# Ten small DRAM transfers per layer move from SyncE's queue to ScalarE's, and the planner's rules for them change

## The chip, the cores and the metric

The kernel runs on one core of a Trainium2 chip. The metric is the device time of one execution in microseconds. An execution uses five engines: TensorE (PE, matrix products; its weight loads are shown apart as PEld), VectorE (DVE), ScalarE (ACT), GpSimd (POOL) and SyncE (SP). SP does no arithmetic here: its instructions issue DMA transfers. A DMA can be issued from ACT's instruction stream as well.

## The reference, cut to what matters

The program is two layers of two blocks each over 256 tokens of 1024 features. Block 1 has differential attention, a gated delta rule in both directions and an MLP, all behind an adaLN vector; block 2 has windowed attention and experts. The change sits in the gated delta rule, which needs the inverse T of a unit lower triangular matrix of 64 by 64 for every head, chunk and direction:

```python
decay = jnp.where(incl, jnp.exp(jnp.where(incl, gdiff, 0.0)), 0.0)
kb = k * beta[..., None]
L = jnp.where(strict, jnp.einsum('bhncd,bhnmd->bhncm', kb, k) * decay, 0.0)
T = lax.linalg.triangular_solve(eye + L, jnp.broadcast_to(eye, L.shape), left_side=True,
                                lower=True, unit_diagonal=True)
u = jnp.einsum('bhncm,bhnme->bhnce', T, v * beta[..., None])
w = jnp.einsum('bhncm,bhnmd->bhncd', T, kb * jnp.exp(g)[..., None])
...
(then a scan over the chunks with u, w and a state)
```

## The kernel before, in words

All products with weights run in two fp32r halves. Weights come in units of 1 MB by `SY.dma_start`; ACT rounds a half of a unit (128x1024) to its high part, DVE subtracts it to get the low part, and PE takes both in products written `ps<-quarter,block` in the profile. A unit thus needs two ACT and two DVE operations before PE can use all of it. These operations are called hi splits and lo splits below.

The inverse is computed in `deltanet` in these steps, once per layer:

- C^T, the strict triangle, comes from two DVE products (one per direction, `quarter<-quarter,quarter`). Four DMAs write it to a DRAM tensor `lb`, one for each direction and half of the partitions.
- One DMA reads the 16x16 blocks on the diagonal back, one per partition (`w<-lb`; the tile is `lt` in the code). DVE copies them (`COPY w<-w 64x256`), and 30 small DVE products and subtractions invert them. The result and its transpose are called X; the last step is a DVE copy (`COPY quarter<-quarter 128x256`).
- One DMA writes X to a DRAM tensor `xd`, and four read it back in block diagonal form (`w<-xd`). Four DVE products make the first T of them, and PE goes from 16x16 to 64x64 blocks with products of 64 rows.

So there are ten small DMAs in a layer, twenty in all. In the kernel before they are written as `SY.dma_start`, and SP issues them in one row with the weight loads.

The order on every engine comes from a planner (`Plan`). Operations are recorded in program order; `keys` gives each its distance to the end by a schedule that runs backwards, and `schedule` then lets each engine take the ready operation with the longest way to go. Other work of the layer that does not need the inverse (gate, attention, adaLN products) is woven into the same block of operations, so a change of one key can move operations on all engines. In the kernel before, all DMAs go through one line in the planner: a DMA starts after the DMA before it is done (`dma = max(t + DMA_START, dma) + o.dma`, line 557). Block 1 of both layers is planned in this way. The order in which operations are issued is then fixed in the program; each engine runs its own row in that order and waits on semaphores.

Of the kernel before, what the change touches and what calls it, by code (L numbers as in the profile page):

```python
# [20 lines left out]
NEG = -1e30  # L21
# [11 lines left out]
# ---------------------------------------------------------------- host layout  # L33
def _units(w, n=2):
    """[K, N] -> [N/(128 n), 128 (k in chunk), n, K/128, 128]: lhsT units of n column chunks."""
    k, c = w.shape
    a = w.reshape(k // 128, 128, c // (128 * n), n, 128).transpose(2, 1, 3, 0, 4)
    return np.ascontiguousarray(a).reshape(c // (128 * n), 128, -1)


def _rows(w, kc):
    """[K, N] -> [K/(128 kc), 128, kc, N]: rhs units of kc row chunks."""
    k, c = w.shape
    a = w.reshape(k // (128 * kc), kc, 128, c).transpose(0, 2, 1, 3)
    return np.ascontiguousarray(a).reshape(k // (128 * kc), 128, -1)


def _cols(v):
    """[n*128] -> [128, n]"""
# [14 lines left out]
def _shape_consts():  # L64
    """constants of the program, packed by the time that they are needed: c0 always, c1 and c2 per block"""
# [71 lines left out]
def _bias(rpb):  # L137
    """[4, 15, 31] -> [4, 128 (q in tile), 2 * 256]: bias of q over k, NEG outside q's window"""
# [92 lines left out]
def _rows_n(w, n):  # L231
    """[1024, N] -> [N/n, 128, 8, n]"""
# [5 lines left out]
# ---------------------------------------------------------------- order of issue  # L238


class Ref:
    """an access pattern of a tile that gets its place when its operations are issued"""
# [28 lines left out]

class Tile:
# [7 lines left out]
class Plan:  # L280
    """Operations are recorded in program order and issued in the order of a list schedule: each engine takes,
    among the operations whose operands are there, the one with the longest way to the end. Costs and latencies
    are the guide's, in ns; they depend on shapes alone. A tile's slot is given out ahead of program order only if
    program order could still go on from there. Products that fill half of the array or less are not issued in long
    rows while others are ready: the array's clock falls when it is used little."""
# [17 lines left out]
    # -------------------------------------------------------- recording  # L303
    def engine(self, key, eng):
        plan = self

        class Proxy:
            def __getattr__(self, name):
                return lambda *a, **k: plan.add(key if name != "dma_start" else "S", name, getattr(eng, name), a, k)
# [16 lines left out]
    def box(r):  # L326
        """(what, partitions from, to, columns from, to)"""
# [37 lines left out]
    def add(self, eng, name, fn, args, kw):  # L365
# [4 lines left out]
        if eng == "P" and self.cols(ins[0]) < 128 and name == "matmul":  # L370
            p = self.ops[-1]
            rng = outs[0].ap.ap[0][1], outs[0].ap.offset // outs[0].ap.ap[0][0]
            if p.group and p.outs[0].t is outs[0].t and rng not in p.group:
                p.group.append(rng)
                self.access(p, n - 1, ins, outs)
                p.calls.append((fn, args, kw))
# [10 lines left out]
        o.eng, o.calls, o.dma, o.deps, o.succ, o.start, o.tiles = eng, [(fn, args, kw)], None, set(), [], None, []  # L387
        if eng == "S":
            b = self.cols(outs[0] if isinstance(outs[0], Ref) else ins[0])
            o.dma, o.dur = max(50.0, 1.4224 * b), 450.0  # L390
            if not isinstance(ins[0], Ref) and ins[0].tensor.name in self.W:
                o.dma = 3.5 * b
        else:
# [32 lines left out]
    # -------------------------------------------------------- scheduling  # L426
# [3 lines left out]
    def keys(self, n0):  # L430
        """time to the end by a list schedule that runs backwards, in which every engine is single"""
# [9 lines left out]
        for _ in range(n0, n):  # L441
# [10 lines left out]
            if o.dma:  # L452
# [12 lines left out]
    def schedule(self, slots):  # L465
        """slots: per kind of tile, the time at which each slot gets free"""
# [24 lines left out]
        def fit(e, t, dur):  # L491
            """the first time from t on at which engine e is idle for dur"""
# [8 lines left out]
        def can(i, t):  # L501
            """the earliest time from t on at which operation i's tiles have slots"""
# [16 lines left out]
        while len(order) < n - n0:  # L519
# [36 lines left out]
            if o.dma:  # L556
# [15 lines left out]
        for e, q in self.busy.items():  # L572
            q += [(ops[i].start, ops[i].end) for i in order if ops[i].eng == e]
# [5 lines left out]
    def flush(self, place, slots, issue):  # L579
        """schedules what has been recorded, into what waits and has gaps; place(kind, slot): the slot's memory"""  # L580
# [8 lines left out]
        for i, place in self.waiting:  # L589
# [5 lines left out]
            for fn, args, kw in o.calls:  # L595
# [1546 lines left out]
```

## Time and profile before

| | us |
|---|---|
| three runs | 2407.43, 2407.26, 2403.64 |
| median | 2407.26 |
| span of the profiled execution | 2408.3 |
| PE busy in it | 1984.8 (82%) |
| DVE busy | 1159.4 (48%) |
| ACT busy | 786.9 (33%) |
| POOL busy | 465.6 (19%) |

The profiled execution is known by its span alone; the span is 1.0 us above the median of the three runs. Layer 0's delta rule lies at about 140 to 340 us of the span, layer 1's at about 740 to 960 us. Block 2 starts behind the two blocks 1, at about 1330 us. All instructions of the program but the last branch stand on line 596 in this profile, because one helper issues them; so operations are told apart by engine, name and shape. The profile gives names of buffers, not those of the code: tiles of 512 columns are `quarter`, small ones `w`, weight units `block`.

### The profile page before, as it was taken

To read this page: it belongs to the slowest core of one execution; us is meant where nothing else is said; L and a number is where in the kernel's file an instruction comes from. 1 tells how busy PE (TensorE), PEld (TensorE's weight loads), DVE (VectorE), ACT (ScalarE), POOL (GpSimd) and SP (SyncE) were. 2 spreads that over 40 slices of the span, in tenths; PEclk is the share of its full clock that TensorE was granted. 3 is DMA by queue.
4 is the path that set the end of the run, shared out by engine and by line. 5 is a ranking of instruction groups with operands and counts; after the bars stand their busy time and mean duration, and the time that the engine had idled before them with its cause. 6 is when DMAs were issued, how large, how long until landed. Compare 5 with 4: busy or idle time off the path is not lost. (4 is left out here: it accounts for less than half of the span.)

```text
span 2408.3 us, 38449 instructions
## 1 busy us (share of the span) xinstructions
PE 1984.8 (82%) x16200; PEld 1437.7 (60%) x16200; DVE 1159.4 (48%) x1908; ACT 786.9 (33%) x1508; POOL 465.6 (19%) x278
## 2 busy tenths in 40 slices
PE   8688987778989999999999887666769988666665
PEld 5677777777987777999986542222237644222222
DVE  5998478999789623775557410000006731000001
ACT  4363343433457323654456210000015521000001
POOL 1555354455133312000020210000002111000000
PEclk7897898788999768999999888887779988877777
DMA  8354224566633310645544699999995579999997
GB/s 315 124 188 128 105 106 158 210 229 254 237 121 132 116 36 18 247 158 178 203 153 167 274 420 420 421 421 420 421 420 212 209 281 420 420 421 420 420 421 313
DMA packets 108253, 622.36 MB, mean 258 GB/s; under 512 B 27184, under 2 KB 28464, under 8 KB 34992
## 3 DMA queue, kind: packets, MB, share of 16 engines
q1 hardware_dynamic: 108080, 619.90, 65.4%
q8 instruction: 127, 2.08, 0.3%
q14 instruction: 46, 0.38, 0.0%
HBM read 617.24 MB, written 2.62 MB: 257 GB/s over the span
## 5 line engine op out<-in xcount | busy, mean ns | idle before, releaser
L596 PE MATMUL ps<-quarter,block 128*128 128x256 f32 (+1 forms) x5760 | 868.4, 304 | 72.5 <-DVE quarter L596 23.6
L596 PEld LDWEIGHTS ps<-quarter,block 128*128 128x128 f32 x5760 | 786.2, 205 | 114.9 <-issue 28.2
L596 PE MATMUL ps<-block,block 128*32 128x256 f32 (+4 forms) x5204 | 546.5, 431 | 137.9 <-DMA block<-in_w_up_dram 95.1
L596 PEld LDWEIGHTS ps<-block,block 128*32 128x32 f32 (+2 forms) x5204 | 274.4, 136 | 354.7 <-DMA block<-in_w_up_dram 159.3
L596 DVE TENSOR_TENSOR block<-block,block 128x1024 fp32r<-128x1024 f32 (+2 forms) x262 | 364.7, 1398 | 130.6 <-PE ps L596 73.1
L596 ACT ACTIVATE block<-block 128x1024 fp32r<-128x1024 f32 (+2 forms) x312 | 319.1, 1028 | 321.9 <-PE ps L596 292.8
L596 ACT ACTIVATE w<-ps 128x256 f32<-128x256 f32 (+1 forms) x138 | 52.3, 382 | 819.0 <-PE ps L596 818.9
L596 DVE TENSOR_TENSOR w<-w,ps 128x256 f32<-128x256 f32 x64 | 26.9, 421 | 544.3 <-ACT w L596 537.8
L596 POOL TENSOR_TENSOR block<-block,block 128x1024 fp32r<-128x1024 f32 x46 | 117.0, 2551 | 794.3 <-ACT block L596 387.8
L596 PE MATMUL ps<-block,w 128*32 128x256 f32 x2048 | 176.0, 500 | 25.8 <-ACT w L596 13.3
L596 PE MATMUL ps<-quarter,quarter 64*64 64x64 f32 (+6 forms) x1312 | 166.8, 304 | 6.9 <-DVE quarter L596 6.9
L596 PEld LDWEIGHTS ps<-block,w 128*32 128x32 f32 x2048 | 76.9, 142 | 116.2 <-issue 49.8
L596 PEld LDWEIGHTS ps<-quarter,quarter 64*64 64x64 f32 (+3 forms) x1312 | 113.2, 177 | 53.2 <-issue 20.0
L596 ACT ACTIVATE quarter<-quarter 128x512 f32<-128x512 f32 (+2 forms) x188 | 116.2, 628 | 85.0 <-DVE quarter L596 82.5
L596 ACT ACTIVATE quarter<-ps 128x512 f32<-128x512 f32 (+1 forms) x136 | 79.5, 592 | 151.2 <-PE ps L596 133.8
L596 DVE SCALAR_TENSOR_TENSOR w<-block,cT,w 128x256 f32<-128x256 f32 x140 | 126.5, 903 | 2.2
L596 DVE TENSOR_SCALAR w<-c,slot 128x256 f32<-128x256 f32 x32 | 12.5, 411 | 234.9 <-PE ps L596 234.8
L596 PE MATMUL ps<-w,w 32*128 32x256 f32 x512 | 106.7, 418 | 15.4 <-ACT w L596 15.1
L596 POOL TENSOR_TENSOR block<-block,cT 128x2048 f32<-128x2048 f32 x20 | 76.5, 3825 | 136.8 <-DVE w L596 41.0
L596 PEld LDWEIGHTS ps<-w,w 32*128 32x128 f32 x512 | 55.5, 185 | 69.2 <-issue 35.4
L596 DVE TENSOR_TENSOR quarter<-quarter,ps 128x512 f32<-128x512 f32 (+1 forms) x80 | 49.0, 629 | 84.7 <-PE ps L596 80.0
L596 POOL TENSOR_TENSOR block<-block 128x1024 f32<-128x1024 f32 (+1 forms) x40 | 85.2, 2131 | 2.4
(169 smaller groups left out, 1604.8 us busy)
## 6 DMA issues: line engine op xcount, KB each, us to landing
block<-in_w_gate_dram SPq DMA_DIRECT2D x144, 1024.0 KB, 19.8
block<-in_w_up_dram SPq DMA_DIRECT2D x128, 1024.0 KB, 19.8
block<-in_w_down_dram SPq DMA_DIRECT2D x128, 1024.0 KB, 19.8
block<-in_w_m_dram SPq DMA_DIRECT2D x64, 1024.0 KB, 4.8
block<-in_ada_dram SPq DMA_DIRECT2D x40, 1024.0 KB, 6.1
block<-in_w_dn_dram SPq DMA_DIRECT2D x16, 1024.0 KB, 4.8
block<-in_w_o_dram SPq DMA_DIRECT2D x16, 1024.0 KB, 7.0
block<-in_w_in_dram SPq DMA_DIRECT2D x12, 1024.0 KB, 12.1
```

The lines of the kernel that those rows point to most:

```text
L596: self.tc.keep_in_program_order(fn(*map(real, args), **{k: real(v) for k, v in kw.items()}))
```

## The change

The proxy of an engine no longer sends every `dma_start` to SP; `SC.dma_start` stays in ACT's row. The ten calls in `deltanet` become `SC.dma_start`. The planner handles a DMA of ACT apart: it takes 60 ns of ACT's time in the plan, and lands after its own latency, outside the line of weight loads. The diff, without removed comments and without a helper that gives every instruction the line of its call (so the kernel after shows true lines in a profile, and its line numbers are up to 29 higher):

```diff
     def engine(self, key, eng):
...
             def __getattr__(self, name):
-                return lambda *a, **k: plan.add(key if name != "dma_start" else "S", name, getattr(eng, name), a, k)
+                return lambda *a, **k: plan.add(key, name, getattr(eng, name), a, k)
...
-        if eng == "S":
+        if name == "dma_start":
             b = self.cols(outs[0] if isinstance(outs[0], Ref) else ins[0])
             o.dma, o.dur = max(50.0, 1.4224 * b), 450.0
             if not isinstance(ins[0], Ref) and ins[0].tensor.name in self.W:
                 o.dma = 3.5 * b
+            if eng == "A":
+                o.dur = 60.0
...
-            if o.dma:
+            if o.dma and o.eng == "A":
+                o.key, at[e] = t + o.dma + self.DMA_START, t + o.dur
+            elif o.dma:
                 dma = max(t, dma) + o.dma
                 o.key = dma + self.DMA_START
...
-            if o.dma:
+            if o.dma and o.eng == "A":
+                o.end = t + self.DMA_START + o.dma
+            elif o.dma:
                 o.end = dma = max(t + self.DMA_START, dma) + o.dma
...
-            q += [(ops[i].start, ops[i].end) for i in order if ops[i].eng == e]
+            q += [(ops[i].start, ops[i].start + ops[i].dur) for i in order if ops[i].eng == e]
...
-                        SY.dma_start(o, CT[d][hv[a]])
+                        SC.dma_start(o, CT[d][hv[a]])
...
-                SY.dma_start(b16(lt), bass.AP(tensor=lb.tensor, offset=lb.offset,
+                SC.dma_start(b16(lt), bass.AP(tensor=lb.tensor, offset=lb.offset,
...
-                SY.dma_start(xd.rearrange("x p c -> p x c"), xb.rearrange("p (x c) -> p x c", x=2))
+                SC.dma_start(xd.rearrange("x p c -> p x c"), xb.rearrange("p (x c) -> p x c", x=2))
...
-                        SY.dma_start(t16[x][d].rearrange("p (q j) -> p q j", q=8), src)
+                        SC.dma_start(t16[x][d].rearrange("p (q j) -> p q j", q=8), src)
```

The number of instructions on every engine stays the same but for the twenty DMAs. The order of block 1 changes on all engines; block 2's hardly does.

SP's row in layer 0, before: rows 61 to 72 of its order, with the four writes of `lb` between weight loads, and the read `w<-lb` behind them.

```order
L596 DMA block_1390<-in_w_gate_dram 128x2048 [waits DMAHW7_49,DVE_49]
L596 DMA lb_106<-quarter_1_1438 64x8x64 [waits DVE_49]
L596 DMA block_1465<-in_w_gate_dram 128x2048 [waits DMAHW1_49,DVE_49]
L596 DMA lb_106<-quarter_1_1438 64x8x64
L596 DMA block_1501<-in_ada_dram 128x2048 [waits DMAHW2_49,DMAHW0_49,DVE_49]
L596 DMA lb_106<-quarter_1_1446 64x8x64
L596 DMA block_1549<-in_w_gate_dram 128x2048 [waits DMAHW4_49,DVE_49]
L596 DMA lb_106<-quarter_1_1446 64x8x64 [waits DMAHW3_49]
L596 DMA block_1590<-in_w_gate_dram 128x2048 [waits Pool_49]
L596 DMA block_1610<-in_ada_dram 128x2048 [waits DMAHW5_49,DVE_49]
L596 DMA block_1629<-in_w_gate_dram 128x2048 [waits DMAHW6_49,DVE_49,Pool_49]
L596 DMA w_7_1636<-lb_106 128x16x16 [waits DMAHW3_49,DMAHW7_49,DMAHW1_49,PE_49]
```

The same place in SP's row after holds weight loads alone, rows 61 to 67:

```order
L778 DMA block_1451<-in_w_gate_dram 128x2048 [waits DMAHW7_49,DVE_49]
L778 DMA block_1488<-in_w_gate_dram 128x2048 [waits DMAHW1_49,DVE_49]
L778 DMA block_1519<-in_ada_dram 128x2048 [waits DMAHW2_49,DVE_49]
L778 DMA block_1588<-in_w_gate_dram 128x2048 [waits DMAHW3_49,Pool_49]
L778 DMA block_1596<-in_w_gate_dram 128x2048 [waits DMAHW5_49,DVE_49]
L778 DMA block_1664<-in_ada_dram 128x2048 [waits DMAHW6_49,DMAHW7_49,DVE_49,Pool_49]
L778 DMA block_1674<-in_w_gate_dram 128x2048 [waits DMAHW0_49,DVE_49]
```

The five small DMAs left SP's row; a weight load there is no longer behind any of them.

ACT's row after, layer 0: the writes of `lb` stand at rows 128, 134, 139 and 145, and these are rows 143 to 151, with the last write, the read of `lb` and its wait for four DMAs.

```order
L1623 ACTIVATE quarter_1_1531<-ps_67,v_0_240 128x512 [waits Pool_49]
L1307 ACTIVATE quarter_1_1536<-ps_87 128x512
L1287 DMA lb_106<-quarter_3_1423 64x8x64 [waits DMAHW3_49]
L882 ACTIVATE quarter_1_1545<-quarter_1_1531 32x512 [waits Activation_49]
L798 ACTIVATE block_486<-block_1451 128x1024 [waits DMAHW5_49,PE_49]
L882 ACTIVATE quarter_1_1545<-quarter_1_1531 32x512
L798 ACTIVATE block_502<-block_1451 128x1024 [waits PE_49]
L1294 DMA w_0_1573<-lb_106 128x16x16 [waits DMAHW4_49,DMAHW6_49,DMAHW3_49,DMAHW0_49]
L1495 ACTIVATE t_1527<-t_1527 128x2 [waits DVE_49]
```

ACT's row before at the same work, rows 143 to 149, has the activations alone:

```order
L596 ACTIVATE quarter_1_1552<-ps_91 128x512 [waits DMAHW7_49,DMAHW5_49,Pool_49]
L596 ACTIVATE quarter_3_1557<-quarter_2_1543 32x512 [waits Activation_49]
L596 ACTIVATE t_1506<-t_1506 128x2 [waits DVE_49]
L596 ACTIVATE quarter_3_1557<-quarter_2_1543 32x512
L596 ACTIVATE block_502<-block_1465 128x1024 [waits DMAHW6_49,PE_49]
L596 ACTIVATE quarter_3_1557<-quarter_2_1543 32x512
L596 ACTIVATE block_485<-block_1465 128x1024 [waits PE_49]
```

ACT now takes the DMAs' semaphore waits in its own row; a hi split (`block<-block`) stands ahead of them and others behind.

DVE's row before, layer 0, rows 258 to 265: inside the inversion of the 16x16 blocks (`w_13`, `quarter_1_1785`) stand the two lo splits of the fourth gate unit (`block_1590`).

```order
L596 TENSOR_TENSOR quarter_1_1785<-quarter_1_1785,w_13_1794 128x12x4 [waits DVE_49]
L596 COPY t_1866<-t_949 64x4
L596 TENSOR_TENSOR block_491<-block_1590,block_518 128x1024 [waits DMAHW4_49,Activation_49]
L596 TENSOR_TENSOR w_13_1794<-w_5_1778,quarter_1_1785 128x55 [waits DVE_49]
L596 COPY t_1866<-t_949 64x4
L596 TENSOR_TENSOR quarter_1_1785<-quarter_1_1785,w_13_1794 128x11x5 [waits DVE_49]
L596 TENSOR_TENSOR block_485<-block_1590,block_485 128x1024 [waits Activation_49]
L596 TENSOR_TENSOR w_13_1794<-w_5_1778,quarter_1_1785 128x60 [waits DVE_49]
```

DVE's row after, layer 0, rows 270 to 279: the lo splits of the fourth gate unit (`block_1596`) stand around the copy that ends X (line 1319).

```order
L1316 TENSOR_TENSOR w_8_1642<-w_6_1625,quarter_2_1632 128x15 [waits DVE_49]
L1526 TENSOR_REDUCE t_1899<-ps_83 128x2 [waits PE_49]
L1318 TENSOR_TENSOR quarter_2_1632<-quarter_2_1632,w_8_1642 128x15 [waits DVE_49]
L800 TENSOR_TENSOR block_495<-block_1596,block_495 128x1024 [waits DMAHW5_49,Activation_49]
L1319 COPY quarter_2_1632<-quarter_2_1632 128x256 [waits DVE_49]
L1527 TENSOR_SCALAR t_1899<-t_1899 128x4
L1386 TENSOR_TENSOR quarter_2_1934<-quarter_1_1536,t_691 128x512
L800 TENSOR_TENSOR block_486<-block_1596,block_486 128x1024 [waits Activation_49]
L1526 TENSOR_REDUCE t_1960<-ps_91 128x2 [waits PE_49]
L1398 COPY t_1971<-t_824 64x4 x2
```

The end of X moved from row 289 to row 274 of DVE, the two products for C^T from rows 193 and 194 to 182 and 183, and the copies of `lt` from row 240 to row 209. In layer 1 the end of X moved from row 911 to 902, C^T from 831 and 832 to 825 and 826, and the copies of `lt` from row 857 to 855. On PE, the first product of the inverse stands 26 of the products `ps<-quarter,block` earlier in layer 0 (747 of them ahead of it, not 773) and 28 earlier in layer 1 (3675, not 3703).

## Rows read from the trace of the kernel before

**Rows 1.** The page's head and its chain that ended last.

```profile
span 2408.3 us, 38449 instructions
...
DMA 17%; PE 5%; ACT 1%; DVE 1%; issue 0%; DVEq 0%; SPq 0%; ACTq 0%
```

**Rows 2.** Windows: start:end, length, busy us by engine, granted clock, DMA share, GB/s.

```profile
150.00:210.00 60.00, 43.65 (x268) 38.50 (x268) 58.75 (x74) 31.46 (x48) 37.60 (x22) 0.82 0.47 152
210.00:340.00 130.00, 122.24 (x923) 95.32 (x922) 80.87 (x136) 49.64 (x101) 51.34 (x39) 0.85 0.34 118
340.00:620.00 280.00, 220.71 (x1609) 207.39 (x1610) 261.13 (x305) 103.10 (x166) 134.87 (x58) 0.87 0.54 207
740.00:820.00 80.00, 71.33 (x475) 62.31 (x473) 78.39 (x119) 48.82 (x73) 35.57 (x24) 0.92 0.44 152
820.00:960.00 140.00, 140.00 (x851) 102.75 (x852) 42.68 (x89) 41.90 (x87) 20.54 (x23) 0.72 0.11 35
960.00:1210.00 250.00, 245.95 (x2003) 243.31 (x2002) 166.31 (x225) 131.14 (x194) 10.75 (x6) 0.99 0.54 193
```

**Rows 3.** The tile lb: who waited for it (us, times).

```profile
  POOL quarter L596: 0.5, 1
```

**Rows 4.** Timeline of SP, layer 0: start, duration, instruction.

```profile
154.18 0.34 SPq L596 DMA_DIRECT2D block<-in_w_gate_dram  x1
154.58 0.59 SPq L596 DMA_DIRECT2D lb<-quarter  x1
...
176.90 0.39 SPq L596 DMA_DIRECT2D w<-lb  x1
...
217.87 0.38 SPq L596 DMA_DIRECT2D xd<-quarter  x1
220.27 2.37 SPq L596 DMA_DIRECT2D w<-xd  x4
```

**Rows 5.** DMA issues from 145 to 230 us: count, size, median us to landing.

```profile
lb<-quarter SPq DMA_DIRECT2D x4, 128.0 KB, 5.1
xd<-quarter SPq DMA_DIRECT2D x1, 256.0 KB, 2.3
w<-xd SPq DMA_DIRECT2D x4, 64.0 KB, 2.5
w<-lb SPq DMA_DIRECT2D x1, 128.0 KB, 7.4
```

**Rows 6.** Timeline of ACT: start, duration, instruction, idle before and its releaser.

```profile
168.75 0.20 ACT L596 ACTIVATE t<-t 128x2 f32<-128x2 f32 x1 [4.22 <-DVE w L596]
...
216.53 0.47 ACT L596 ACTIVATE quarter<-ps,t 128x256 f32<-128x256 f32 x1 [14.40 <-DVE t L596]
...
824.91 1.06 ACT L596 ACTIVATE block<-block 128x1024 fp32r<-128x1024 f32 x1 [10.59 <-PE ps L596]
```

**Rows 7.** Timeline of DVE, layer 0, from C^T to the end of X.

```profile
148.45 3.49 DVE L596 TENSOR_TENSOR quarter<-quarter,quarter 128x512 f32<-128x512 f32 x2
...
189.97 0.69 DVE L596 COPY w<-w 64x256 f32<-64x256 f32 x2
...
196.41 4.05 DVE L596 TENSOR_TENSOR quarter<-quarter,t 128x512 f32<-128x512 f32 x1
...
203.95 3.32 DVE L596 TENSOR_TENSOR block<-block,block 128x1024 fp32r<-128x1024 f32 x1
...
209.47 1.21 DVE L596 TENSOR_TENSOR block<-block,block 128x1024 fp32r<-128x1024 f32 x1
...
214.81 0.68 DVE L596 TENSOR_REDUCE t<-ps 128x2 f32<-128x512 f32 x1
...
217.46 0.39 DVE L596 COPY quarter<-quarter 128x256 f32<-128x256 f32 x1
```

**Rows 8.** Timeline of PE, layer 0, just before X is done.

```profile
195.29 2.27 PE L596 MATMUL ps<-quarter,block 128*128 128x256 f32 x17
...
207.32 5.06 PE L596 MATMUL ps<-quarter,block 128*128 128x256 f32 x22 [6.93 <-DVE block L596]
```

More of the change, by code (lines that the diff above doesn't have):

```diff
@@ L1 @@
 import math
+import sys
 from bisect import bisect
@@ L269, in real, with line, call_at @@
         return x
+HELPERS = {"act", "tt", "ts", "stt", "mm", "sigm", "<lambda>"}
+CALLS = {}
+def line():
+    f = sys._getframe(2)
+    while f.f_code.co_name in HELPERS:
+        f = f.f_back
+    return f.f_lineno
+def call_at(n):
+    if n not in CALLS:
+        space = {}
+        exec(compile("\n" * (n - 1) + "def call(fn, a, k): return fn(*a, **k)", __file__, "exec"), space)
+        CALLS[n] = space["call"]
+    return CALLS[n]
 class Tile:
@@ L375, in add @@
                 self.access(p, n - 1, ins, outs)
-                p.calls.append((fn, args, kw))
+                p.calls.append((fn, args, kw, line()))
                 if len(p.group) == 2:
@@ L386, in add @@
             o.small = name == "matmul" and min(k, n_) <= 64
-        o.eng, o.calls, o.dma, o.deps, o.succ, o.start, o.tiles = eng, [(fn, args, kw)], None, set(), [], None, []
-        if eng == "S":
+        o.eng, o.calls, o.dma, o.deps, o.succ, o.start, o.tiles = eng, [(fn, args, kw, line())], None, set(), [], None, []
+        if name == "dma_start":
             b = self.cols(outs[0] if isinstance(outs[0], Ref) else ins[0])
@@ L594, in flush @@
             real = lambda x: x.real() if isinstance(x, Ref) else x
-            for fn, args, kw in o.calls:
-                self.tc.keep_in_program_order(fn(*map(real, args), **{k: real(v) for k, v in kw.items()}))
+            for fn, args, kw, n in o.calls:
+                self.tc.keep_in_program_order(
+                    call_at(n)(fn, tuple(map(real, args)), {k: real(v) for k, v in kw.items()}))
         self.waiting = []
```

## The prediction

> **What bounds the kernel now.** I first read the page's head and the chain of work that ended last [rows 1]. The chain is almost DMA alone, 17% of the span, and lies wholly in block 2, which streams weights. It does not say what block 1 is worth. But block 2 begins when block 1 ends, so whatever delays or shortens block 1 moves the end of the program one for one. The question is then what sets block 1's end, and that is read from the busy time by window [rows 2]. In layer 0, from 150 to 210 us, DVE is busy 58.75 of 60 us, while PE is idle 16.35 us and ACT 28.54 us: DVE sets the pace. From 210 to 340 us, PE is busy 122.24 of 130 us and DVE only 80.87: PE sets it, with 7.76 us of idle time left. From 340 to 620 us DVE is busy 261.13 of 280 again. In layer 1 it is the same picture, sharper: DVE 78.39 of 80 us up to 820 us, then PE without a gap for 140 us, at a mean granted clock of 0.72, and to 1210 us at 0.99 with 4.05 us idle. So a gain needs DVE to finish X earlier and PE to have less left to do behind it, and a transfer matters only if one of the two waits for it.
>
> Then I asked who waits for the small transfers. For `lb`, nobody but POOL, 0.5 us once [rows 3]. For the transfers of `xd` the trace names no waiting engine. In SP's row the small DMAs do stand among weight loads: the second write of `lb` is issued at 154.58 us, right behind a gate load at 154.18 [rows 4]. That load had itself been waiting for a free buffer. The small writes wait for loads, then, and the loads do not wait for them.
>
> **The change part by part.** *SP's time.* Removed from SP and added to ACT in each layer: four writes at 0.59 us, the read of `lb` at 0.39, the write of `xd` at 0.38, and four reads in 2.37 us [rows 4]: 2.36 + 0.39 + 0.38 + 2.37 = 5.50 us, 11.0 us in both layers. SP has nothing to gain, as no load is late. I take 0 for SP. ACT's price for an issue is not in this trace; I take SP's. ACT is idle 28.54 us between 150 and 210 us, and just at X's end it stands 14.40 us before 216.53 us in layer 0 and 10.59 us before 824.91 in layer 1 [rows 6]. The 5.50 us fit in that cover: 0. Without cover it would be +11.0, and below 0 it cannot go.
>
> *Landing.* The write of `lb` took 5.1 us to land and the read 7.4 us [rows 5]. Nothing waited: the read issued at 176.90 landed at about 184.3, and DVE copied `lt` at 189.97 [rows 4, 7], 5.7 us later. An earlier landing is worth 0 by itself.
>
> *The wait that may be new: DVE for `lt`.* The copies of `lt` stood 46 rows behind C^T on DVE and now stand 26 behind. In before those 46 rows took from 151.94 (148.45 + 3.49) to 189.97, 38.0 us [rows 7]; 26 at the same pace take 21.5 us. On ACT, 19 activations lie between the first write of `lb` (row 128) and its read (row 150). Between 150 and 210 us an activation took 31.46/48 = 0.66 us of work, or 60/48 = 1.25 us with ACT's waits [rows 2]. So the read is issued after 12.5 + 2.4 = 14.9 us at the least and 23.8 + 2.4 = 26.2 us at the most, and lands 5.1 to 7.4 us later [rows 5]: 20.0 to 33.6 us. Against 21.5 that is a wait of 0 to 12 us on a full DVE. I take 2, near the lower end, because much of ACT's waiting is for DVE itself (4.22 us before 168.75 [rows 6]) and stretches both sides alike. For layer 1, where the copies stand 29 rows behind C^T instead of 25, I take 0.5.
>
> *DVE up to X.* In layer 0 DVE reaches the end of X 15 rows earlier. What is gone ahead of it is two lo splits and one operation of 512 columns. A split undisturbed is 1.21 us and the reduction over 512 columns 0.68 [rows 7], so 3.1 us. But such operations are stretched there: a split took 3.32 us at 203.95 and an operation of 512 columns 4.05 at 196.41, and with those the sum is 3.32 + 1.21 + 4.05 = 8.6 us. I take 5, between them. In layer 1 two reductions are gone: 2 x 0.68 = 1.4 us.
>
> *PE behind X.* The work is not gone, only behind X. Of the products `ps<-quarter,block`, 26 fewer are done in layer 0 when the inverse begins and 28 fewer in layer 1. One costs 2.27/17 = 0.134 us [rows 8], so 3.5 and 3.7 us come later, where PE sets the end. Part of it fills PE's idle 7.76 us in layer 0; I take half, 1.8. In layer 1 PE has no gap from 820 to 960 us [rows 2], but is idle 8.67 us before that and could use X's earlier end; I take 1.4 of the 3.7 as filled there. The bounds are 0 and the whole: 0 to +3.5, 0 to +3.7. The two lo splits around X are the other side of the same coin: PE stood 6.93 us until such a split let it go on at 207.32, and now it may stand until X's end, 217.85 in before (217.46 + 0.39 [rows 7]), less the 5 us taken above.
>
> *The sum.* Layer 0: -5 (X earlier) + 2 (wait) + 1.8 (PE) = -1.2. Layer 1: -1.4 + 0.5 + (3.7 - 1.4) = +1.4. Together +0.2 us: nothing. The span of the profiled execution is 1.0 us above the median of the runs, so the same sum is set on the median: 2407.26 + 0.2, **2407.5 us**.
>
> **One rule weighed.** The row of the timeline shows small writes issued between weight loads and landing in 5.1 us [rows 4, 5]. The Trainium skill, "DMA: Bandwidth & Descriptors", section "Issuing engines are not separate DMA queues", says that transfers from any engine end up on the same 16 DMA engines and that issuing on another one saves only issue time on the sequencer. That speaks against the change: by it, landing stays at 5.1 and 7.4 us, the sum stays where it is, and ACT only takes over SP's issue time. The same page, "Queues, rings and completion order", has each DMA engine take turns between queue rows packet by packet; if ACT's transfers are in another row they would pass a queued load. By that rule the landing would be shorter, which is the first rival's condition; no run shows a transfer issued by ACT yet.
>
> **The rivals.**
> *Faster, by an earlier inverse.* If the small transfers no longer queue behind loads, and land sooner, DVE has no wait for `lt`, X comes 8.6 us earlier in layer 0, and PE's late work is filled in its idle time. That gives -8.6 + 1.8 = -6.8 in layer 0 and -1.4 + 0 in layer 1: -8.2, 2399 us. For it: 22.3 us pass on SP from the second write of `lb` to its read (154.58 to 176.90 [rows 4]). Against it: nobody waited for them.
> *Faster, by the clock.* From 820 to 960 us PE is full at a granted clock of 0.72 [rows 2]. The new order mixes the 64-row products differently with the others. With 0.77 the 140 us would take 130.9: -9.1, 2398 us. With 0.68 they would take 148.2: +8.2. Nothing in the rows says which way.
> *Slower: ACT stands at X's transfers.* Behind the write of `xd` ACT waits for it to land, 2.3 us, then issues four reads in 2.37 us; with its own 0.38, ACT is shut for 5.1 us per layer, and hi splits for PE's next unit stand right behind. ACT's idle time covers it only if PE has products left at that point. It decides if PE runs out within 5.1 us of X's end, and PE did run out just before, for 6.93 us [rows 8]. Price: 2 x 5.1 = +10.2, 2418 us. Against it: in layer 1 PE was full from 820 us on.
> *Slower: DVE waits for `lt`.* With the middle of its bounds, 6 us in layer 0 rather than 2, and 4 in layer 1: +4 + 3.5 = +7.5, 2415 us.
>
> **How the numbers follow.** What a measurement of this kernel can tell from no change is about 0.2%, 4.8 us. The neutral sum I give 0.37; its own range is 2403 to 2412. An earlier inverse gets 0.23 and a higher clock 0.12, so faster is 0.35. ACT at X's transfers gets 0.15, DVE's wait 0.08 and a lower clock 0.05, so slower is 0.28. For the range, 2393 to 2420 takes in each case alone (2398, 2399, 2415, 2418), but not two of one sign at once.
>
> **What would show it.** In the profile after, SP should hold weight loads only, and the window before X should still show DVE full. Right would be: DVE waits for the read of `lb` at the copies of `lt` for less than 3 us; the end of X lies 1 to 7 us earlier than at 217.85 in layer 0; ACT's idle time before its next work at X, 14.40 us in layer 0, now holds the transfers of `xd`. Wrong on the ACT step would be a PE idle of several us behind X that ends with a hi split; wrong on the neutral sum would be layer 1's stretch of full PE starting earlier than 820 us by more than 4 us or showing a mean clock off 0.72 by more than 0.04. If block 1 starts layer 1 at another time than before, the cause lies in the DVE-bound stretch from 340 to 620 us, which I take as unchanged.

## The result, and the profile after

The changed kernel takes 2438.94 us (median of four runs) against 2405.45 us: a ratio of 1.0145, with a 95% interval of 1.012 to 1.0169. It is slower by 33 us, where almost no change (2407.5 us) was predicted. The prediction was wrong.

The page of the kernel after, its head and the DMA queues (queue, kind: packets, MB, share of 16 engines' span):

```profile
span 2436.7 us, 38474 instructions
...
q1 hardware_dynamic: 90864, 617.54, 64.1%
q10 hardware_dynamic: 17216, 2.36, 0.6%
```

The change does what it says: the small transfers have a queue of their own, q10. The DMA issues of the kernel after from 140 to 230 us (count, size, median us to landing):

```profile
lb<-quarter ACTq DMA_DIRECT2D x4, 128.0 KB, 2.6
xd<-quarter ACTq DMA_DIRECT2D x1, 256.0 KB, 2.1
w<-xd ACTq DMA_DIRECT2D x4, 64.0 KB, 5.9
w<-lb ACTq DMA_DIRECT2D x1, 128.0 KB, 5.6
```

The writes of `lb` land in 2.6 us instead of 5.1 [rows 5]. The reads of `xd` land later, 5.9 us instead of 2.5; that goes with the new order, as they take 5.4 us when SP issues them in it (`plan_only` below). The waits that were feared are small. For the tile `lb` in the kernel after, the row on DVE (us, times), then ACT at X in its timeline:

```profile
  DVE w L1297: 0.8, 1
```

```profile
206.00 0.37 ACTq L1321 DMA_DIRECT2D xd<-quarter  x1
...
209.19 4.81 ACTq L1327 DMA_DIRECT2D w<-xd  x2
214.04 1.06 ACT L798 ACTIVATE block<-block 128x1024 fp32r<-128x1024 f32 x1 [4.69 <-DMA w<-xd]
```

DVE waits 0.8 us once for the read of `lb`, and ACT stands 4.69 us at the reads of `xd`. X is done at 205.96 us instead of 217.85 [rows 7], 11.9 us earlier. So layer 0's X came earlier, as the change would have it, and the kernel still lost 33 us.

Windows of the kernel after at the places of [rows 2] (the columns are the same: busy time and instructions of PE, PEld, DVE, ACT and POOL, then granted clock, DMA share, GB/s):

```profile
150.00:210.00 60.00, 45.58 (x282) 40.36 (x283) 58.45 (x96) 29.65 (x51) 32.69 (x19) 0.86 0.45 156
210.00:340.00 130.00, 123.48 (x825) 89.46 (x825) 66.10 (x99) 41.00 (x80) 52.01 (x40) 0.78 0.28 98
340.00:620.00 280.00, 218.48 (x1573) 204.69 (x1574) 258.44 (x299) 102.73 (x170) 138.65 (x60) 0.85 0.53 199
740.00:820.00 80.00, 76.46 (x544) 66.81 (x541) 72.32 (x113) 52.65 (x85) 27.34 (x17) 0.92 0.37 125
820.00:960.00 140.00, 135.40 (x801) 98.22 (x800) 56.13 (x113) 47.20 (x93) 26.90 (x25) 0.72 0.16 50
```

The second row tells most. PE is as busy as before, 123.48 us to 122.24, but gets through 825 products instead of 923, at a clock of 0.78 instead of 0.85. Busy time alone hides that.

To place the loss, both traces were laid beside each other at equal work: the starts of the 720th, 1080th, ... of the 5760 products `ps<-quarter,block`. Each stage between two of them has the same dense work, but not the same small products: by the traces the inverse of layer 0 begins behind 725 dense products before and 699 after (48 fewer each than the order's 773 and 747, the same difference of 26), so that 128 of its products lie ahead of product 720 after and none before. PE's busy time was split by the granted clock, which is either 1.00 (2.4 GHz) or 0.50 (1.2 GHz):

| products | before: us, idle, at half clock | after: us, idle, at half clock | after - before |
|---|---|---|---|
| 0 to 720 (to X of layer 0) | 231.4, 50.2, 61.6 | 229.8, 49.0, 38.1 | -1.6 |
| 720 to 1080 (inverse, scan) | 145.0, 17.6, 35.4 | 151.6, 14.0, 62.2 | +6.6 |
| 1080 to 2280 | 224.2, 47.4, 43.3 | 227.5, 48.9, 46.5 | +3.3 |
| 2280 to 2880 | 75.8, 1.2, 0.0 | 82.0, 4.8, 4.4 | +6.2 |
| 2880 to 3120 (norm of layer 1) | 45.2, 6.0, 6.5 | 55.7, 12.6, 15.1 | +10.5 |
| 3120 to 3480 | 77.2, 4.7, 3.2 | 78.3, 3.5, 6.5 | +1.1 |
| 3480 to 3960 (inverse, scan of layer 1) | 189.0, 5.6, 86.9 | 188.3, 4.9, 87.9 | -0.7 |
| 3960 to 5759 | 226.8, 3.8, 3.3 | 227.9, 3.5, 6.6 | +1.1 |

That is 26.5 us of the 28.4 between the two spans. The stages in which the small transfers are issued changed by -1.6 us (layer 0), +1.1 and -0.7 (layer 1). Half-clock time costs little where PE has to wait anyway: up to product 720 it fell by 23.5 us, and the stage by 1.6. From there on it rose by 50.6 us, by estimate worth 25 us if that work runs at half speed, and idle time by 5.9; the stages from there lost 28.1.

How half clock looks in layer 0, in windows of 15 us: first the kernel before, then the kernel after.

```profile
285.00:300.00 15.00, 15.00 (x109) 14.24 (x107) 5.63 (x6) 8.32 (x11) 3.84 (x2) 0.91 0.53 192
300.00:315.00 15.00, 15.00 (x88) 11.80 (x87) 11.60 (x20) 10.20 (x25) 6.95 (x4) 0.89 0.38 146
315.00:330.00 15.00, 13.10 (x132) 10.39 (x130) 11.29 (x16) 5.72 (x15) 12.06 (x10) 1.00 0.19 72
```

```profile
285.00:300.00 15.00, 12.52 (x86) 10.00 (x85) 13.89 (x19) 10.10 (x22) 8.18 (x4) 0.96 0.28 91
300.00:315.00 15.00, 14.76 (x60) 9.53 (x60) 3.10 (x8) 5.09 (x13) 2.04 (x2) 0.50 0.29 121
315.00:330.00 15.00, 15.00 (x58) 9.50 (x58) 3.43 (x6) 2.25 (x5) 4.92 (x4) 0.63 0.20 72
```

From 300 to 330 us PE is busy 29.8 us after and 28.1 before, but does 118 products at 0.50 and 0.63 after, where it did 220, not quite of the same kinds, at 0.89 and 1.00 before. What PE runs there in the kernel after, from its timeline:

```profile
307.35 0.58 PE L840 MATMUL ps<-quarter,block 128*128 128x256 f32 x1
307.86 0.70 PE L1432 MATMUL ps<-quarter,quarter 128*64 128x128 f32 x4
308.49 0.58 PE L839 MATMUL ps<-quarter,block 128*128 128x256 f32 x1
309.00 0.69 PE L1432 MATMUL ps<-quarter,quarter 128*64 128x128 f32 x4
```

One dense product and four of the scan's take turns, 1.14 us a round. What such turns can explain is that PE stays at half clock. What came first is an idle gap: the clock fell at 298.71 us, inside the gap ahead of this product, and stayed low to 326.02.

```profile
300.24 1.22 PE L1553 MATMUL ps<-quarter,quarter 128*128 128x256 f32 x2 [2.73 <-ACT quarter L1451]
```

The longest such stretch of the kernel before in this stage, from 253.64 to 270.70 us, has a gap of 2.96 us just ahead of it:

```profile
252.87 0.33 PE L596 MATMUL ps<-quarter,quarter 64*64 64x64 f32 x4 [2.96 <-DVE quarter L596]
```

In layer 1's scan no gap is needed: in the kernel after PE is busy without one when the clock falls at 858.5 us, for 61.4 us, and dense and small products had taken turns at full clock since 852.6. Two windows around that fall:

```profile
845.00:860.00 15.00, 15.00 (x54) 10.72 (x54) 3.70 (x4) 3.83 (x10) 2.64 (x2) 0.73 0.51 139
860.00:875.00 15.00, 15.00 (x95) 9.79 (x94) 8.89 (x17) 4.00 (x6) 5.95 (x7) 0.50 0.01 2
```

### The profile page after: what moved, and what is told of

It reads as the page before. It is cut to its first block, busy times and chain, and to the rows that moved or that the text cites. A ratio compares the mean times of both kernels' runs of the same rounds, so it can differ in the third digit from the quotient of the medians.

```text
span 2436.7 us, 38474 instructions
## 1 busy us (share of the span) xinstructions
PE 2008.4 (82%) x16200; PEld 1445.5 (59%) x16200; DVE 1155.8 (47%) x1908; ACT 784.2 (32%) x1508; POOL 472.5 (19%) x278
## 5 line engine op out<-in xcount | busy, mean ns | idle before, releaser
L839 PE MATMUL ps<-quarter,block 128*128 128x256 f32 x1856 | 489.5, 304 | 29.7 <-DVE x L1673 8.8
L840 PE MATMUL ps<-quarter,block 128*128 128x256 f32 x1856 | 489.6, 305 | 8.9 <-DVE quarter L1666 6.5
L2108 PE MATMUL ps<-block,block 128*32 128x256 f32 x4096 | 345.7, 455 | 135.6 <-DMA block<-in_w_up_dram 95.2
L842 PE MATMUL ps<-quarter,block 128*128 128x256 f32 x1856 | 442.9, 305 | 8.8 <-DVE block L800 8.8
L800 DVE TENSOR_TENSOR block<-block,block 128x1024 fp32r<-128x1024 f32 (+1 forms) x258 | 359.1, 1399 | 144.4 <-PE ps L842 66.4
L798 ACT ACTIVATE block<-block 128x1024 fp32r<-128x1024 f32 (+1 forms) x296 | 308.5, 1049 | 307.0 <-PE ps L840 210.8
L839 PEld LDWEIGHTS ps<-quarter,block 128*128 128x128 f32 x1856 | 348.6, 204 | 47.8 <-issue 24.6
L840 PEld LDWEIGHTS ps<-quarter,block 128*128 128x128 f32 x1856 | 347.2, 204 | 26.3 <-issue 8.0
L842 PEld LDWEIGHTS ps<-quarter,block 128*128 128x128 f32 x1856 | 343.8, 204 | 23.3 <-DVE block L800 9.4
L2108 PEld LDWEIGHTS ps<-block,block 128*32 128x32 f32 x4096 | 116.4, 123 | 327.1 <-DMA block<-in_w_up_dram 162.8
L800 POOL TENSOR_TENSOR block<-block,block 128x1024 fp32r<-128x1024 f32 x38 | 99.1, 2615 | 807.1 <-ACT block L798 727.3
L2111 ACT ACTIVATE w<-ps 128x256 f32<-128x256 f32 x32 | 12.3, 384 | 516.0 <-PE ps L2108 498.4
L2131 PE MATMUL ps<-w,w 32*128 32x256 f32 x512 | 105.5, 415 | 15.4 <-ACT w L2127 15.1
L971 DVE SCALAR_TENSOR_TENSOR w<-block,cT,w 128x256 f32<-128x256 f32 x140 | 113.0, 808 | 2.0
L964 POOL TENSOR_TENSOR block<-block,cT 128x2048 f32<-128x2048 f32 x20 | 76.0, 3802 | 130.0 <-DVE w L971 32.1
L2127 ACT ACTIVATE w<-ps 128x256 f32<-128x256 f32 x32 | 12.3, 384 | 202.5 <-PE ps L2124 202.5
L2116 PE MATMUL ps<-c,w 128*128 128x128 f32 x64 | 19.0, 386 | 64.6 <-DVE w L2113 63.4
```

The costliest lines, as they stand in the source:

```text
L798: act(hi, r[:, h * n:h * n + n])
L800: tt(lo, r[:, h * n:h * n + n], f(hi), OP.subtract, e[self.ns % len(e)])
L839: mm(o, hi[:, j, k], xhi(k), k == 0, False)
L840: mm(o, hi[:, j, k], xlo(k), False, False)
L842: mm(o, lo[:, j, k], xhi(k), False, k == kc - 1)
L964: tt(r, r, bcl(cT, 256), OP.mult, G)
```

## The experiments

Two theories stood at the start. **P**: the loss lies in the re-planned order. **Q**: it lies in ACT's queue. The planner and the queue can be taken apart, since SP's rules can be kept while ACT issues, and the other way round. The ratio of each kernel is to runs of the kernel before on the same chip.

**The queue alone** (`queue_only`): the four lines with these calls in the kernel before (one of them is shown), nothing else; PE, DVE and GpSimd keep their order.

```diff
-                        SY.dma_start(o, CT[d][hv[a]])
+                        SC.dma_start(o, CT[d][hv[a]])
```

> The order of the kernel before on every engine, with the twenty small DMAs issued from ACT at their places in the total order. Theory P (the loss of 33 us is in the re-planned order): within 4 us of before, about 2405 us, since ACT has 14 us of idle time at X and nobody waits for the transfers. Theory Q (the loss is ACT standing at DMA waits): 2425 to 2440 us. A gain of more than 5 us would say that the queue itself helps and the plan hides it.

Measured: 2412.73 us, 1.002 (0.9996 to 1.0044). The median is 6.0 us above that of before, a little outside theory P's 4 us and far from theory Q's 18 or more; the interval takes in no change as well as a cost of 0.44%. Its ACT timeline at X shows that a queue shared with computation delays transfers too:

```profile
214.91 0.37 ACTq L596 DMA_DIRECT2D xd<-quarter  x1
...
225.54 0.60 ACT L596 ACTIVATE quarter<-ps 128x512 f32<-128x512 f32 x1 [8.22 <-PE ps L596]
225.54 0.37 ACTq L596 DMA_DIRECT2D w<-xd  x1
```

The first read of `xd` is issued only when an activation ahead of it is released by PE, 10.6 us after the write; SP issued it 2.4 us after [rows 4]. A hi split stands behind these DMAs, and PE waits for it:

```profile
229.68 0.85 PE L596 MATMUL ps<-quarter,block 128*128 128x256 f32 x5 [1.93 <-ACT block L596]
```

From 230.51 us PE is at half clock for 47.8 us. Products 720 to 1080 take 151.3 us, 58.5 of them at half clock, where the kernel before has 145.0 and 35.4. So in this one layer the queue alone does what the table above shows for the kernel after (151.6 and 62.2).

**The plan alone** (`plan_only`): the kernel after, its small DMAs issued from SP. All other orders stay those of after.

```diff
-                return lambda *a, **k: plan.add(key, name, getattr(eng, name), a, k)
+                return lambda *a, **k: plan.add(key, name, getattr(eng if name != "dma_start" else plan.nc.sync, name), a, k)
```

> The order of the kernel after on every engine, with the twenty small DMAs issued from SP at their places in the total order. Theory P: as after, 2434 to 2442 us. Theory Q: as before, 2400 to 2412 us. If loads on SP are held up behind the small DMAs, more than after, up to 2450 us.

Measured: 2440.08 us, 1.0141 (1.0119 to 1.0163). Theory P is shown: the order alone gives the whole loss, and theory Q falls as its cause. Stage by stage, with SP's queue in both kernels, the order alone costs 10.7 us in products 720 to 1080 (155.6 us, 73.8 at half clock), 4.7 in 2280 to 2880, 10.0 at layer 1's norm and 3.4 in 3480 to 3960.

**A re-plan for no reason** (`vv128`, `ds1050`): the kernel before with one number of the planner changed: DVE's latency 127 to 128, or `DMA_START` 1100 to 1050.

> The kernel before, all DMAs on SP, with one latency of the planner (DVE to DVE) 128 ns instead of 127: block 1 is re-planned without any reason in the hardware. Theory L (before's order is a good one among its neighbours, and any re-plan costs): 2412 to 2440 us. Theory S (the rules for ACT's DMAs are what makes the order bad): within 5 us of before, 2400 to 2410 us.

Measured: 2406.75 us, 1.0008 (0.9995 to 1.002). Its order differs from before's in 25 operations on DVE, so it hardly is another plan and tells little.

> The kernel before, all DMAs on SP, with the planner's time from a DMA's issue to its start 1050 ns instead of 1100. Theory L: 2412 to 2440 us. Theory S: 2400 to 2410 us.

Measured: 2448.86 us, 1.0172 (1.0155 to 1.0189). Here the order is another one throughout, no DMA left SP, and the loss is at least the change's own, above theory L's range too. Theory S falls: the loss needs no rule for ACT's DMAs. That any re-plan costs, as theory L says, does not hold either: three re-plans further down gain.

**One layer at a time** (`l0_rules`, `l1_rules`): in the kernel after, only the DMAs of one layer get the new rules.

```diff
-                return lambda *a, **k: plan.add(key, name, getattr(eng, name), a, k)
+                return lambda *a, **k: plan.add(key if name != "dma_start" or any(x.tensor.name[:3] in ('lb0', 'xd0') for x in a if not isinstance(x, Ref)) else "S", name, getattr(eng, name), a, k)
```

> All twenty small DMAs issued from ACT; the planner's rules for ACT's DMAs for layer 0 alone, so that layer 0 has nearly the order of the kernel after and layer 1 nearly that of before. Local theory (each layer's new order costs its own part, as the lag of the dense products shows: about 14 us by the end of layer 0's MLP, 12 us in layer 1): 2415 to 2425 us, with the lag at dense product 2400 at +10 to +15 us and no more added in layer 1. Layer 1 theory (what costs is layer 1's order alone): 2404 to 2412. If the loss of layer 0 is given back: below 2410.

> All twenty small DMAs issued from ACT; the planner's rules for ACT's DMAs for layer 1 alone, so that layer 0 has the order of before. Local theory: 2415 to 2425 us, the lag zero to +5 us up to dense product 2400, and about 12 us added behind it. Layer 0 theory (the lag is made in layer 0 and only moves on): 2404 to 2412 us.

Measured: 2422.71 us, 1.0072 (1.0049 to 1.0095) for layer 0, and 2430.97 us, 1.0097 (1.008 to 1.0114) for layer 1. The first is in the range expected, the second 6 us above it. Each layer's order costs its own part: 0.52% and 0.77% over the queue alone, which with its 0.2% come to 1.49% against 1.45% measured for all of it; but 0.2% is itself not told from nothing. In the trace of `l1_rules` products 2880 to 3120 take 55.2 us, and in that of `l0_rules` 45.8: that loss belongs to layer 1's order. That stage takes 53.0 to 55.7 us in all eight kernels with after's rules in layer 1 or the order of `ds1050`, and 44.2 to 45.8 in the nine others. Layer 0's scan is less clear: `l1_rules` has before's order there, with ACT's queue, and takes 151.0 us with 59.0 at half clock, like `queue_only` and behind the same kind of gap (1.80 us, for a hi split of ACT).

**The bound on rows of small products** (`small0`, `small2000`): the planner lets half-array products run in a row up to a bound of 1000 ns, and then prefers full ones. The kernel after with another bound:

```diff
-    SMALL = 1000.0
+    SMALL = 0.0
```

> The kernel after with the planner's bound on rows of half-array products at 0 instead of 1000 ns: whenever such a product was issued, a full one is taken next if one is ready. Clock theory (layer 0's loss is PE at half clock in the scan, 62 us of half-clock work where before had 35): less half-clock time there, 2420 to 2436 us. Idle theory (the loss is waiting in the chain of the scan): no change or slower, 2436 to 2450 us, since spacing lengthens the chain.

> The kernel after with the planner's bound on rows of half-array products at 2000 ns instead of 1000: longer rows of them. Clock theory: more half-clock time in layer 0's scan and 2442 to 2460 us. Idle theory: same or faster than after, 2430 to 2440 us.

Measured: 2491.64 us, 1.0352 (1.033 to 1.0374) at 0 ns, and 2426.63 us, 1.0077 (1.006 to 1.0095) at 2000 ns. Both times lie outside both ranges. The theory behind both expectations fell: spacing the small products out makes PE slower, and leaving them together makes it faster. In layer 0's scan the clock moves with it: products 720 to 1080 had 104.4 us at half clock and took 176.0 us at 0 ns, and 48.8 us and 141.5 us at 2000 ns.

**The norm of layer 1** (`clear`, `clear2`). In the stage 2880 to 3120, PE is idle longest before one product: 1.02 us in the kernel before, 5.92 us in the kernel after, in this order:

```profile
685.22 0.30 PE L596 MATMUL ps<-quarter,w 128*32 128x256 f32 x1 [1.02 <-ACT quarter L596]
```

```profile
705.45 0.42 PE L1145 MATMUL ps<-quarter,w 128*32 128x256 f32 x1 [5.92 <-ACT quarter L1082]
```

DVE's timeline of the norm in the kernel after has two lo splits (line 800) in it, and its small operations take 2.60 and 2.53 us; in the kernel before, such ones took 0.43. First a row of the kernel before, then the kernel after:

```profile
683.68 0.43 DVE L596 SCALAR_TENSOR_TENSOR w<-w,w 128x256 f32<-128x256 f32 x1
```

```profile
695.57 2.06 DVE L800 TENSOR_TENSOR block<-block,block 128x1024 fp32r<-128x1024 f32 x1 [1.28 <-ACT block L798]
697.56 2.60 DVE L873 TENSOR_TENSOR w<-w,w 128x256 f32<-128x256 f32 x1
700.20 0.43 DVE L874 TENSOR_TENSOR w<-w,w 128x256 f32<-128x256 f32 x1
700.73 2.53 DVE L875 SCALAR_TENSOR_TENSOR w<-w,w 128x256 f32<-128x256 f32 x1
703.18 1.21 DVE L800 TENSOR_TENSOR block<-block,block 128x1024 fp32r<-128x1024 f32 x1
704.32 2.06 DVE L1081 SCALAR_TENSOR_TENSOR w<-x,t,w 128x256 f32<-128x256 f32 x5
```

`clear` moves the two splits in the issue order until the next operation that needs them or their slots, which puts one right behind the first scaled x (706.32 us) and one 6.4 us further on; `clear2` also lets DVE do two splits there that GpSimd did beside the norm.

```diff
+        for p in [p for p in at["lo"] if a + 8 < p < b][::-1]:
+            z, q = W[p], p
+            o = ops[z[0]]
+            if o.eng == "G":
+                o.calls = [(self.nc.vector.tensor_tensor, x, kw, l) for _, x, kw, l in o.calls]
...
+                W[q] = W[q + 1]
...
+        self.clear()
```

(`clear` has not the two lines on `o.eng`.)

> The kernel after, with the two lo splits that DVE does inside layer 1's first norm moved behind the norm's first results; GpSimd's row is unchanged. Chain theory (the two splits, and GpSimd's splits beside them, stretch the norm from 2.8 to 10.7 us and PE stands for it): from the norm's first DVE operation to the first scaled x 3 to 6 us, PE's idle time in dense products 2880 to 3120 down from 12.6 to 6 to 9 us, and 5 to 9 us less than after: 2429 to 2434 us. Rival (PE is short of split weights there, so the splits are needed where they stand): no gain, 2437 to 2442 us.

> As the kernel with the two splits moved, and the two lo splits that GpSimd does in the same stretch are done by DVE, behind the norm's first results. If GpSimd's operations stretch DVE's by themselves: the norm takes 3 us and the kernel is 1 to 3 us below the one with the two splits moved. If only the splits in DVE's row cost: the same as that one or slower by up to 3 us, since DVE has two operations of 1.2 us more.

Measured: 2441.99 us, 1.014 (1.0106 to 1.0174), and 2438.51 us, 1.0123 (1.008 to 1.0166). The norm did shrink, from 10.7 us to 6.3 and 4.3, but the stage only from 55.7 us to 53.4 and 53.0, and no gain can be told: `clear` is where the rival expected it, and the two medians differ by less than their intervals. PE's idle time moved on, as its rows in `clear` show:

```profile
707.06 0.31 PE L1169 MATMUL ps<-quarter,w 128*32 128x256 f32 x1 [1.57 <-ACT quarter L1106]
711.66 0.42 PE L1169 MATMUL ps<-quarter,w 128*32 128x256 f32 x1 [4.17 <-DVE quarter L1107]
```

5.74 us in two pieces instead of 5.92 in one. The chain theory falls in this form: moved out of the norm's first operations, the splits stand among the scaled x, and PE waits for those. An order that has them done earlier was not tried.

The pair shows one more thing, about DVE and GpSimd. The last small operation of the norm on DVE, first in `clear`, with the GpSimd operation beside it, then in `clear2`, where GpSimd has nothing to do at that time:

```profile
703.38 2.43 DVE L899 SCALAR_TENSOR_TENSOR w<-w,w 128x256 f32<-128x256 f32 x1
```

```profile
702.85 2.68 POOL L824 TENSOR_TENSOR block<-block,block 128x1024 fp32r<-128x1024 f32 x1 [0.32 <-ACT t L1121]
```

```profile
705.31 0.42 DVE L901 SCALAR_TENSOR_TENSOR w<-w,w 128x256 f32<-128x256 f32 x1
```

The same operation takes 2.43 us and ends 0.28 us after GpSimd's split (705.81 against 705.53), or it takes 0.42. The Trainium skill, "SBUF — State Buffer", section "SBUF: two separate sides", has the two engines share a pair of ports that one instruction holds to its end; the pair of kernels agrees.

**The bound in the kernel before** (`before_small1500`, `before_small2000`): the same one-line edit, on the kernel before.

> The same with 1500 ns: 19 of DVE's operations move against before. Small re-plan: within 6 us of before, 2400 to 2412 us; if longer rows help by themselves, 2396 to 2404 us.

> The kernel before (all DMAs on SP) with the planner's bound on rows of half-array products at 2000 ns instead of 1000. If longer rows of such products leave PE less at half clock, as in the kernel after with the same edit (272 us of half-clock time where 0 ns had 363): 2395 to 2405 us, faster than both kernels. If any new plan loses what before's plan has by luck: 2412 to 2435 us.

Measured: 2393.4 us, 0.9934 (0.9911 to 0.9957), and 2372.73 us, 0.9854 (0.9824 to 0.9884). Both are faster than any range expected. With 2000 ns the kernel beats before and after: its windows in layer 0 run at full clock where the others fell.

```profile
255.00:270.00 15.00, 15.00 (x124) 11.43 (x124) 5.95 (x15) 8.47 (x19) 7.58 (x8) 1.00 0.26 81
270.00:285.00 15.00, 15.00 (x116) 14.15 (x115) 6.26 (x7) 7.57 (x10) 2.62 (x1) 1.00 0.58 221
285.00:300.00 15.00, 14.08 (x89) 10.78 (x88) 13.06 (x21) 9.93 (x23) 6.85 (x5) 1.00 0.39 151
300.00:315.00 15.00, 15.00 (x153) 12.37 (x153) 10.77 (x17) 6.76 (x19) 12.54 (x9) 1.00 0.30 111
```

**Three runs on what was open**: whether the mixing of products is the cause whatever made the plan, and what the queue is worth on a plan without that loss.

> The kernel before (DMAs on SP, its own rules) with the planner's bound on rows of half-array products at 0 ns. PE changes between the delta rule's products and dense products 563 times in its row, where before does it 417 times and after 517. Mixing theory (the changes of form keep PE at half clock, whatever made the plan): half-clock time in dense products 720 to 1080 and 3480 to 3960 above that of after (62 and 88 us), and 2450 to 2500 us. Rival (after's rules for the DMAs make the loss, and the bound matters only with them): 2400 to 2420 us.

> The kernel before with the bound at 5000 ns; 399 changes of form, where 2000 ns has 403 and ran 2373 us. Mixing theory: 2365 to 2385 us. If the gain of 2000 ns was a single lucky order: 2390 to 2415 us.

> The order of before with the bound at 2000 ns, with the twenty small DMAs issued from ACT at their places in the total order: the change's queue alone, on another plan. If the queue is neutral: within 5 us of the one issued from SP, 2368 to 2378 us. If ACT's standing at the DMAs costs 5 us, as the median of the first such pair (2412.7 against 2406.7) suggests: 2376 to 2384 us.

Measured: 2478.45 us, 1.0283 (1.0254 to 1.0312) for `before_small0`; 2375.45 us, 0.9868 (0.9822 to 0.9913) for `before_small5000`; 2378.58 us, 0.9875 (0.9851 to 0.9898) for `queue_small2000`. Without any rule for ACT's DMAs, 0 ns loses 68 us, and 5000 ns confirms 2000. The mixing theory's ranges hold, that for the clock too: `before_small0` has 89.9 and 132.8 us at half clock in the two stages. The queue alone is again at or a little behind SP's row, 0.9875 to 0.9854, with overlapping intervals.

`queue_only` and `queue_small2000` make a close pair. Both have the order of before and ACT's queue, and issue the same work on every engine up to one place, where the longer bound lets a row of the inverse's products go on. PE's rows, first in `queue_only`, then in `queue_small2000`, each with a window of 15 us further on (columns as above):

```profile
231.79 1.55 PE L596 MATMUL ps<-quarter,quarter 64*64 64x64 f32 x24
...
245.00:260.00 15.00, 15.00 (x106) 10.38 (x105) 7.02 (x9) 0.41 (x1) 5.91 (x2) 0.50 0.21 71
```

```profile
229.29 0.86 PE L596 MATMUL ps<-quarter,block 128*128 128x256 f32 x5 [1.80 <-ACT block L596]
...
231.33 1.98 PE L596 MATMUL ps<-quarter,quarter 64*64 64x64 f32 x32
...
245.00:260.00 15.00, 15.00 (x169) 10.83 (x168) 8.47 (x9) 3.80 (x10) 10.76 (x7) 1.00 0.37 137
```

Both fall to half clock right behind the gap, at 230.5 and 230.2 us. With 24 products in the row PE stays there for 47.8 us, with 32 for 3.4, and then runs single dense products in turn with four small ones at full clock. By this pair the order behind the gap decides how long PE stays at half clock, and turns as such do not bring the clock down at once. It is one execution of each; `l1_rules`, which has `queue_only`'s order there, stayed for 47.8 us as well.

All kernels in one table. "Changes" counts the stretches of one kind in PE's row, of products of the delta rule and attention (`ps<-quarter,quarter`) and of dense ones (`ps<-quarter,block`); the changes between them are one fewer. The half-clock and idle time of PE run to the last dense product, as does the third time. These three are of the profiled execution, the median is of all executions:

| kernel | changes | half clock, us | idle, us | last dense product, us | median, us |
|---|---|---|---|---|---|
| before_small2000 | 403 | 183 | 128 | 1179 | 2372.73 |
| before_small5000 | 399 | 192 | 124 | 1179 | 2375.45 |
| queue_small2000 | 403 | 177 | 127 | 1173 | 2378.58 |
| before_small1500 | 401 | 215 | 130 | 1197 | 2393.4 |
| before | 417 | 240 | 137 | 1215 | 2405.45 |
| vv128 | 417 | 219 | 135 | 1209 | 2406.75 |
| queue_only | 417 | 263 | 133 | 1221 | 2412.73 |
| l0_rules | 469 | 242 | 134 | 1221 | 2422.71 |
| small2000 | 513 | 272 | 138 | 1235 | 2426.63 |
| l1_rules | 465 | 275 | 139 | 1237 | 2430.97 |
| clear2 | 517 | 300 | 134 | 1249 | 2438.51 |
| after | 517 | 267 | 141 | 1241 | 2438.94 |
| plan_only | 517 | 289 | 137 | 1245 | 2440.08 |
| clear | 517 | 294 | 136 | 1247 | 2441.99 |
| ds1050 | 517 | 293 | 140 | 1253 | 2448.86 |
| before_small0 | 563 | 327 | 121 | 1277 | 2478.45 |
| small0 | 551 | 363 | 130 | 1291 | 2491.64 |

Idle time hardly moves and, in the slowest two, goes against the time. Half-clock time rises with the time, over 180 us of it, and orders with more changes have more of it. Both hold broadly and not row by row: 417 changes come with 219 to 263 us at half clock, `small2000` has no less of it than after and is 12 us faster, and `l1_rules` has more with fewer changes. No run changed the number of changes and nothing else, so that it is the changes which hold the clock down, and not something else in these orders, is argued and not shown.

## Why the prediction was wrong, point by point

The step that failed took the new order to be worth no more than the products moved at X, 3.5 and 3.7 us, with the clock and all other stages as before. That order by itself costs 1.41% (`plan_only`), the whole loss.

- **SP's time at 0, landing at 0: right in the new order.** The plan alone and the plan with the queue are the same (1.0141 and 1.0145), while the writes of `lb` landed in 5.0 us from SP and 2.6 from ACT. The rule weighed, of the Trainium skill, "DMA: Bandwidth & Descriptors", section "Issuing engines are not separate DMA queues", agrees with the time; that landing stays as it is, as the prediction drew from it, does not come true, as 2.6 us differs from 5.0 in the same order. In before's order ACT's part may not be 0: two pairs of kernels have it 0.2% slower (1.002, and 0.9875 to 0.9854), neither clear of noise.
- **DVE's wait for `lt`: right,** 0.8 us, where 2 was taken.
- **DVE up to X: right in sign, too small.** X came 11.9 us earlier in layer 0; 5 was taken, with a bound of 8.6. In layer 1 X is done 17.7 us behind dense product 3480 instead of 25.5; 1.4 was taken.
- **PE behind X: the first step that failed.** The moved products were priced at 0.134 us each, a price at full clock, with 0 to 3.5 us as bounds, and the clock of everything else behind X at nothing. The stage from 720 to 1080 has 26.8 us more at half clock, 13.4 us if at half speed, and lost 6.6 us although X was early and 128 of the inverse's products lay ahead of it. With SP's queue the order alone lost 10.7 there; with ACT's queue before's order lost 6.3 as well, so in the changed kernel this stage is not the order's alone. The prediction spoke of the mix of products only as a rival for layer 1, and said that nothing in the rows tells which way. The order gives a hint: 417 changes of form became 517.
- **The sum covered two places only: the second step that failed.** It held what lies around the transfers, and took the rest as unchanged. The order of block 1 differed on every engine, and 10.5 us went at layer 1's norm, 6.2 us in the stage before it, with no small DMA near. This is the larger part, and it is the order's: 10.0 and 4.7 us with SP's queue. At the norm 6.6 us are idle time of PE and 8.6 us more at half clock.
- **The rival "ACT stands at X's transfers": it happened, and in the changed kernel no loss shows at it.** ACT stood 4.69 us in layer 0 once, with X 11.9 us early. In before's order its sign, a PE idle that ends with a hi split, is there in layer 0 (1.93 us in `queue_only`); what follows costs 6.3 us in that stage by the clock, where 5.1 a layer was priced. The rival on the clock named the mechanism, but with 0.05 for a loss and only for layer 1's scan, where the stage from 3480 to 3960 lost nothing in the changed kernel (87.9 us at half clock for 86.9) and 3.4 us in `plan_only` (97.9); most of the half-clock time came in layer 0.

What stays open: what in an order holds the clock down, why it falls in layer 1's scan without a gap, and what in the new order put the norm's splits so late. That before's order has 35 us at half clock in products 720 to 1080 in one profile and 58 in another goes with the queue as far as the profiles tell: 35.4 and 32.1 from SP (before, and `vv128` with nearly its order), 58.5 and 59.0 from ACT (`queue_only`, `l1_rules`).

## What to carry to other kernels

When a change touches the keys of a planner, price the whole new order and not the edit: look at every stage where the rows moved, and count on PE's row how often it changes between kinds of products, as a hint to the clock. Look for the gaps of PE ahead of each stretch at half clock. A full PE is no measure of work; put the granted clock and the number of products beside its busy time. And before a change of queue is blamed or praised, run its order with the old queue, and the old order with its queue.

## What the runs showed that was not expected

- A lower bound on rows of half-array products was expected to keep the clock up. On both kernels 0 ns gave more half-clock time: 363 us against 272 at 2000 in the kernel after, 327 against 183 in the kernel before. One number was worth 1.46%, as much as the change lost.
- A transfer issued from ACT's row can be late because ACT waits for PE: the reads of `xd` were issued 10.6 us after the write in `queue_only`.
- In the same order the writes of `lb` landed in 2.6 us from ACT and 5.0 from SP, but the read `w<-lb` in 5.6 and 2.9. What decides between them was not tried.
